# Moving gathered second layers beside the gates, and the second tile's dots beside the dense second layers

## The chip, the cores and the metric

One core of a Trainium2 chip runs the whole program. The metric is the device time of one execution in microseconds (us). A profile of one execution shows what each engine did: TensorE (PE for matmuls, PEld for weight loads), VectorE (DVE), ScalarE (ACT), GpSimd (POOL) and the queues, of which SP loads weights, ACT moves intermediate results, and POOL issues the gathers.

## What is computed

Two transformer blocks run one after the other on 512 tokens of width 1024. The change lies in the last part of the second, a layer that finds single-neuron experts by product keys. Each token has 8 heads with 16 picks each, so 128 experts out of 16384, each with a gate:

```python
def peer_ffn(h, w_query, keys1, keys2, expert_u, expert_v):
    ...
    top_s, top_pos = lax.top_k(cand_s, PEER_TOPK)
    idx = jnp.take_along_axis(cand_i, top_pos, axis=-1)
    gate = jax.nn.softmax(top_s.astype(jnp.float32), axis=-1).astype(h.dtype)
    ...
    def block(args):
        hb, ib, gb = args
        act = jax.nn.gelu(jnp.einsum('thkd,td->thk', expert_u[ib], hb), approximate=False)
        return jnp.einsum('thk,thkd->td', gb * act, expert_v[ib])
```

expert_u and expert_v are 16384 x 1024 in float32, 64 MB each.

## The kernel before, in words

phase_d does this layer. It treats the 512 tokens as four tiles of 128 and in two ways.

Tiles 0 and 1 (NS = 2) are *fetching* tiles. For each token its 128 rows of u are gathered: gather n brings one row of 1024 floats to each of the 128 partitions (L1346), and VectorE multiplies it with the token's own row and sums it into one column of dots (L1355, a "dot"). After 128 dots ScalarE takes Gelu and the product with the gate (L1357, L1358) gives gg. Then the second layer: step r of a tile gathers four sets of rows of v (one for each group of 32 tokens) and multiplies them on the PE with z, which holds gg transposed (L1377, L1378) so that one block of 32 columns picks one token per row (L1384). A tile has 32 such steps of 4 gathers and 8 matmuls; I call them V steps. Their sums stand in two PSUM tiles os.

Tiles 2 and 3 (256 tokens, ND) are *dense*: all 16384 experts are computed. In 128 chunks n, the PE multiplies a chunk of u with the tokens (u_chunk, L1328), ScalarE takes Gelu. The first 68 chunks (JR) stay in SBUF as ge, the other 60 go to DRAM as st and come back as gl. A gate must be multiplied into each; the gates are built from one-hot matrices by VectorE and ScalarE in 64 gate steps (gates, L1299 to L1315), on the PE as small matmuls pg (L1309); the part for st goes to DRAM as gdr. At last, in 128 dense steps, the PE multiplies a chunk with the rows of v of that chunk (L1495) into four PSUM tiles o.

So there are two stages. In the *gates stage* (loop over n) the PE does the chunks of u, pulls the routing of tiles 2 and 3 (rt) until n = 68, then one gate step for each n; beside it the chain ga of both tiles' dots is pulled 200 times in 128 chunks (GU = 200), six more before. Then `early.close()` frees the pools ep and ps, and in the *dense stage* (loop over i) each i does one dense step, pulls one dot until i = 60, and every odd i pulls one V step, 64 in all (rows_left).

The order on each engine comes from a scheduler that simulates the program as it is written down; a generator that is pulled writes its instructions at that point. In the dense stage the PE's order is the written one (manual_schedule). POOL, SP and ACT issue in order, so a gather that waits holds up all behind it. A row buffer is free again when its dot, or its V step, is done: six buffers in pool sb, and six more in pool lp in the dense stage. lp lies in SBUF that ep had, so its tiles wait for what lay there. hr is the residual (tokens before the layer), loaded into one buffer of lp and added by the PE with the identity (residual, L1339), for tiles 2 and 3 inside the first dense step.

Of the kernel before, what the change touches and what calls it, by code (L numbers as in the profile page):

```python
# [11 lines left out]
FT = mybir.dt.float32  # L12
# [11 lines left out]
D = 1024  # L24
# [1091 lines left out]
def phase_d(k):  # L1116
# [14 lines left out]
    with ExitStack() as ctx:  # L1131
# [5 lines left out]
        ps = early.enter_context(tc.tile_pool(name="d_ps", bufs=1, reuse_waits="tile", space=PS))  # L1137
        def pm(tag="a", bufs=3):
            return (pg if tag == "g" else ps).tile([128, 512], FT, name="p" + tag, tag=tag, bufs=bufs)
# [4 lines left out]
        cand = ep.tile([128, 8, 112], FT, name="cand")  # L1144
# [9 lines left out]
        xs = [ep.tile([128, 4, N0], FT, name="xs", tag="kept", bufs=3) for _ in range(2)]  # L1154
# [37 lines left out]
        def first(h, s):  # L1192

            w = k.load(I["peer_wq"][h], [128, 8, 256])
            for side in range(2):
                p = pm()
                for c in range(8):
                    nc.tensor.matmul(p[:, 0:256], w[:, c, 128 * side:128 * side + 128],
                                     x[:, c] if s else xs[c // 4][:, c % 4], start=c == 0, stop=c == 7)
                q = ep.tile([128, 256], FT, name="q", bufs=3)  # L1200
# [13 lines left out]
        def second(j):  # L1214
# [28 lines left out]
            pxf = ep.tile([128, 4, 128], F16, name="pxf", bufs=1)  # L1243
# [6 lines left out]
            res = ep.tile([128, 2, 128], FT, name="res", bufs=2)  # L1250
            yield
            for side in range(2):
                tie, eq = (ep.tile([128, 16, 128], F16, name=n, tag="kept", bufs=3) for n in ("tie", "eq"))
# [34 lines left out]
        def gates(ge):  # L1288
# [3 lines left out]
            for tb in range(NG):  # L1292
                gs = ep.tile([128, 2048], FT, name="gs", tag="big")[:, :JL * TB].rearrange("p (j t) -> p j t", j=JL)
                for t4 in range(TB // 4):
                    t0 = tb * TB + 4 * t4
                    p = pm("g", 2)
                    o1, o2, oh, ol = (ep.tile(sh, F16, name=f"o{n}", bufs=2) for n in range(4))
# [52 lines left out]
        def gathered_u(j):  # L1350

            dots = sb.tile([128, 128], FT, name=f"dots{j}")
            for n in range(128):
                r = gather(I["peer_u_rows"], ia[j][:, n:n + 1])
                stt(r, r, 1.0, ht[j], op0=OP.mult, op1=OP.mult, accum_out=dots[:, n:n + 1])  # L1355
                yield
            act(dots, dots, AF.Gelu)  # L1357
            tt(gg[j], dots, gg[j], op=OP.mult)  # L1358

        def gathered_v(z):  # L1360

            rows = {}

            def fetch(n):
                if n < 32 * NS:
                    o = [32 * g + n % 32 for g in range(4)]
                    rows[n] = [gather(I["peer_v"], iat[n // 32][:, i:i + 1]) for i in o]

            for n in range(2):
                fetch(n)  # L1370
            for n in range(32 * NS):
                j, r = n // 32, n % 32
                fetch(n + 2)
                if r == 0:
                    po = [ps.tile([128, 512], FT, name=f"os{i}", tag=f"os{i}") for i in range(2)]
                    p = pm("g", 2)
                    nc.tensor.transpose(p[:, 0:128], gg[j], k.ident)  # L1377
                    act(z.rearrange("p (g y) -> p g y", g=4)[:, :, 0::33],  # L1378
                        p[:, 0:128].rearrange("p (g r) -> p g r", g=4), AF.Copy)
                rs = rows.pop(n)  # L1380
                for i in range(2):
                    for g in range(4):
                        o = 1024 * g + 32 * r
                        nc.tensor.matmul(po[i][32 * g:32 * g + 32], z[:, o:o + 32], rs[g][:, 512 * i:512 * i + 512],  # L1384
                                         start=r == 0, stop=r == 31, skip_group_check=True)
                if r == 0:
                    residual(po, j)
                if r == 31:
# [25 lines left out]
        rp.append((sb, 6))  # L1414
# [3 lines left out]
        rt, ga = routing(), chain(*(gathered_u(j) for j in range(NS)))  # L1418
        for j in range(NS):
            for _ in second(j):  # L1420
                pass
            pull(ga, 3)
        taken = [0]

        def some(n):
            taken[0] += n
            pull(ga, n)
# [3 lines left out]
        for n in range(JR + JP):  # L1431
# [4 lines left out]
            else:  # L1436
                i = (n - JR) % JG
                if i == 0:
                    while pull(rt, 1):
                        pass  # L1440
                    kept = ep.tile([128, JG, ND], FT, name="kept", bufs=3)
# [4 lines left out]
            pull(ga, (n + 1) * GU // (JR + JP) - n * GU // (JR + JP))  # L1446
# [10 lines left out]
        z = lp.tile([128, 4096], FT, name="z", bufs=1)  # L1457
        nc.gpsimd.memset(z, 0.0)
# [24 lines left out]
        rows_left = gathered_v(z)  # L1483
# [24 lines left out]
        for j in range(4):  # L1508
            y = sb.tile([128, D], FT, name="rows", bufs=6)
# [162 lines left out]
```

## Time and profile before

| what | us |
|---|---|
| median of three runs | 3017.49 (3016.68 to 3018.36) |
| the profiled execution's own time | 3018.37 |
| its span | 3016.6 |
| PE busy | 2713.6 (90%) |
| VectorE busy | 1224.5 (41%) |
| GpSimd busy | 591.7 (20%) |

The shares are means over stages with different limits. The gates stage and the dense stage are the last 1200 us or so, and their stretches must be read one by one: the column PEclk is the clock that was granted to TensorE as a share of full speed, and a DMA share of about 1.0 means that all of the core's 16 DMA engines had packets all the time.

### The profile page before, as it was taken

What the parts mean: (1) busy time and instruction counts of PE and PEld (TensorE: products, weight loads), DVE (VectorE), ACT (ScalarE), POOL (GpSimd) and SP (SyncE); (2) the same over time, 40 slices, a digit from 0 to 9 for tenths busy, and PEclk for the clock granted to TensorE, in tenths of its full rate; (3) what the DMA queues carried; (4) which work ended last, traced back from release to release, by engine and by line L of the source; (5) the groups of instructions that cost most, each with busy time, mean ns of one, the idle gap of its engine ahead of it and who ended that gap; (6) DMA issues with size and microseconds to landing.
All of it is one profiled execution on the core that took longest, in us unless ns stands there. A gap on an engine that the chain in (4) does not pass through costs nothing. (4 is left out here: it accounts for less than half of the span.)

```text
span 3016.6 us, 35266 instructions
## 1 busy us (share of the span) xinstructions
PE 2713.6 (90%) x13794; PEld 1594.1 (53%) x13794; DVE 1224.5 (41%) x3040; ACT 623.2 (21%) x1304; POOL 591.7 (20%) x600
## 2 busy tenths in 40 slices
PE   8999888887888777699999997999998499999997
PEld 6877422322232222377777786888887333333332
DVE  5444411111111111268855389985888522200001
ACT  4333200000000000265333121122555300000000
POOL 1000100000000000000000005454433256544442
PEclk9979999999999999899999998999999699999999
DMA  4104899999999999912113239999999699999996
GB/s 158 42 1 154 367 421 421 421 421 421 420 421 420 421 421 376 376 60 85 56 56 112 92 132 355 365 381 361 379 363 350 225 399 412 412 410 363 401 401 252
DMA packets 185453, 912.93 MB, mean 303 GB/s; under 512 B 18864, under 2 KB 38464, under 8 KB 112192
## 3 DMA queue, kind: packets, MB, share of 16 engines
q1 hardware_dynamic: 83664, 602.85, 49.7%
q0 software_dynamic: 73728, 268.47, 23.0%
q10 hardware_dynamic: 27888, 39.29, 3.6%
q8 instruction: 110, 1.80, 0.2%
q14 instruction: 63, 0.52, 0.0%
HBM read 890.61 MB, written 19.92 MB: 302 GB/s over the span
## 5 line engine op out<-in xcount | busy, mean ns | idle before, releaser
L1328 PE MATMUL pa<-x,w 128*128 128x256 f32 x2048 | 455.4, 381 | 0.0
L1328 PEld LDWEIGHTS pa<-x,w 128*128 128x128 f32 x2048 | 385.9, 191 | 50.6
L1355 DVE SCALAR_TENSOR_TENSOR rows<-rows,ht 128x1024 f32<-128x1024 f32 x256 | 310.5, 1218 | 237.5 <-DMA rows<-in_peer_u_rows,ia 211.4
L1346 POOL DMA_INDIRECT rows<-in_peer_u_rows,ia x256 | 287.8, 1124 | 440.1 <-DVE rows L1355 211.1
L1346 POOL DMA_INDIRECT rows<-in_peer_v,iat x256 | 253.0, 988 | 292.1 <-PE os L1384 151.1
L712 PE MATMUL pr<-w,xs 128*32 128x512 f32 x1024 | 212.4, 697 | 91.6 <-DMA w<-in_expert_up 91.4
L732 PE MATMUL px<-w,ht 128*32 128x512 f32 x1024 | 223.2, 599 | 44.9 <-DMA w<-in_expert_down 35.5
L1495 PE MATMUL o<-w,ge 128*128 128x512 f32 x544 | 243.4, 600 | 0.0
L1495 PE MATMUL o<-w,gl 128*128 128x512 f32 x480 | 215.5, 602 | 4.4 <-DVE gl L1481 4.4
L71 PE MATMUL pm<-xg,w8h 128*128 128x512 f32 x640 | 206.4, 402 | 3.5 <-ACT cc L942 1.4
L712 PE MATMUL pg<-w,xs 128*32 128x512 f32 x1024 | 178.7, 612 | 19.3 <-DMA w<-in_expert_gate 19.3
L960 POOL MEMSET acc<- 128x1024 f32 x1 | 1.0, 952 | 936.4 <-PE px L732 936.4
L712 PEld LDWEIGHTS pr<-w,xs 128*32 128x32 f32 x1024 | 46.0, 124 | 245.1 <-DMA w<-in_expert_up 168.7
L1495 PEld LDWEIGHTS o<-w,ge 128*128 128x128 f32 x544 | 100.8, 191 | 139.4 <-issue 139.4
L732 PEld LDWEIGHTS px<-w,ht 128*32 128x32 f32 x1024 | 53.4, 109 | 203.0 <-DMA w<-in_expert_down 95.8
L718 DVE SCALAR_TENSOR_TENSOR hd<-pr,ga,hd 128x512 f32<-128x512 f32 x16 | 12.0, 751 | 361.6 <-PE pr L712 361.6
L1495 PEld LDWEIGHTS o<-w,gl 128*128 128x128 f32 x480 | 89.4, 191 | 131.0 <-issue 122.9
L1384 PE MATMUL os<-rows,z 128*32 128x512 f32 x1024 | 144.6, 600 | 5.4 <-DMA rows<-in_peer_v,iat 4.3
L1481 DVE TENSOR_TENSOR gl<-gl,g 128x256 f32<-128x256 f32 x60 | 21.5, 420 | 305.2 <-DMA gl<-st 305.2
L71 PEld LDWEIGHTS pm<-xg,w8h 128*128 128x128 f32 x640 | 120.8, 190 | 33.7 <-ACT w8h L59 2.0
L745 DVE TENSOR_TENSOR hT<-hT,po 128x512 f32<-128x512 f32 x128 | 86.0, 687 | 128.7 <-PE po L744 127.3
L59 ACT ACTIVATE w8h<-w 128x1024 fp32r<-128x1024 f32 (+3 forms) x101 | 90.8, 901 | 218.7 <-PE pm L71 106.3
(561 smaller groups left out, 3601.8 us busy)
## 6 DMA issues: line engine op xcount, KB each, us to landing
w<-in_expert_up SPq DMA_DIRECT2D x128, 1024.0 KB, 19.8
w<-in_expert_gate SPq DMA_DIRECT2D x128, 1024.0 KB, 19.8
w<-in_expert_down SPq DMA_DIRECT2D x128, 1024.0 KB, 19.8
w<-in_peer_u SPq DMA_DIRECT2D x64, 1024.0 KB, 8.1
w<-in_peer_v SPq DMA_DIRECT2D x64, 1024.0 KB, 8.3
w<-in_peer_wq SPq DMA_DIRECT2D x16, 1024.0 KB, 4.8
w<-in_w_out SPq DMA_DIRECT2D x8, 1024.0 KB, 4.8
st<-kept ACTq DMA_DIRECT2D x15, 512.0 KB, 9.3
```

The source lines that it names most:

```text
L59: nc.scalar.activation(hi, src, AF.Copy)
L71: nc.tensor.matmul(o, w[:, c, :], x[:, c, s], start=first and c == 0 and n == 0, stop=last and c == kc - 1 and n == 2)
L712: nc.tensor.matmul(p[s], xs[:, 4 * half + c, s], ws[e][:, c], start=half == 0 and c == 0, stop=half == 1 and c == 3, skip_group_check=True)
L718: stt(hd, pu, ga[:, 1:2], hd, op0=OP.mult, op1=OP.mult)
L732: nc.tensor.matmul(pd[n][s], ht[:, 2 * half + f, s], ws[e][:, f, 512 * n:512 * n + 512], start=half == 0 and f == 0, stop=half == 1 and f ...
L745: tt(hx[:, c], hx[:, c], p, op=OP.add)
L1328: nc.tensor.matmul(p[:, :ND], w[:, c], x[:, c], start=c == 0, stop=c == 7)
L1346: nc.gpsimd.indirect_dma_start(out=r, out_offset=None, in_=rows, in_offset=bass.IndirectOffsetOnAxis(ap=idx, axis=0))
L1355: stt(r, r, 1.0, ht[j], op0=OP.mult, op1=OP.mult, accum_out=dots[:, n:n + 1])
L1384: nc.tensor.matmul(po[i][32 * g:32 * g + 32], z[:, o:o + 32], rs[g][:, 512 * i:512 * i + 512], start=r == 0, stop=r == 31, skip_group_chec ...
L1481: tt(b, b, g[:, :, j], op=OP.mult)
L1495: nc.tensor.matmul(out[NS + t][c], w[:, 128 * t:128 * t + 128], vp[:, i % 2, 512 * c:512 * c + 512], start=i == 0, stop=i == NJ - 1, skip_ ...
```

## The change

Dots and V steps become one generator per tile. In the gates stage only tile 0's dots are pulled (128 instead of 200); when they are used up, each odd n pulls a V step of tile 0. What is left of tile 0 is pulled at odd i of the dense stage, beside all dots of tile 1 (one at each i below 16, then two), and from i = 72 on the V steps of tile 1. For that, V steps must run before `early.close()`:

- z becomes four small tiles per tile of tokens, each for eight steps (z_part). In the gates stage they use the places of ion and cand, which routing no longer needs.
- os gets its own PSUM pool, in place of three banks for routing that are closed when routing is done.
- Row buffers: nine in sb (six before); the space comes from fewer buffers elsewhere ("kept" 2 instead of 3; q, pxf, res and the one-hot tiles share eight "k1" tiles); in the dense stage five more in lp, 14 in all (12 before).
- In the gates stage the matmuls of a V step keep their order by a dependency without a semaphore; each step fetches the rows of the next one (ahead = 1; 2 in the dense stage, as before).
- The residual of a fetching tile is added behind its last V step instead of its first.

```diff
-            act(dots, dots, AF.Gelu)
-            tt(gg[j], dots, gg[j], op=OP.mult)
-        def gathered_v(z):
...
+                if n == 127:
+                    act(dots, dots, AF.Gelu)
+                    tt(gg[j], dots, gg[j], op=OP.mult)
                 yield
+        def z_part(j, r8, pool, tag, bufs):
+            z = pool.tile([128, 4, 8, 32], FT, name="z", tag=tag, bufs=bufs)
+            nc.gpsimd.memset(z, 0.0)
+            p = pm("g", 2)
+            nc.tensor.transpose(p[:, 0:128], gg[j], k.ident)
+            act(z.rearrange("p g r y -> p g (r y)")[:, :, r8:r8 + 232:33],
+                p[:, 0:128].rearrange("p (g r) -> p g r", g=4)[:, :, r8:r8 + 8], AF.Copy)
+            return z
+        def gathered_v(j, zt):
+            rows, z = {}, zt["tiles"]
+            def fetch(r):
+                if r not in rows and r < 32:
+                    rows[r] = [gather(I["peer_v"], iat[j][:, 32 * g + r:32 * g + r + 1]) for g in range(4)]
+            po = [os.tile([128, 512], FT, name=f"os{i}", tag=f"os{i}") for i in range(2)]
+            for r in range(32):
+                for n in range(zt["ahead"] + 1):
+                    fetch(r + n)
+                for r8 in (r - r % 8, r - r % 8 + 8):
+                    if (j, r8) not in z and r8 < 32 and r >= r8 - 4:
+                        z[j, r8] = z_part(j, r8, *zt["z"](r8))
...
-        rp.append((sb, 6))
+        rp.append((sb, 9))
...
-        rt, ga = routing(), chain(*(gathered_u(j) for j in range(NS)))
+        zt = {"tiles": {}, "ahead": 1, "held": True, "z": lambda r8: (ep, ("ion", "cand")[r8 // 8 % 2], 1)}
+        rt, ga, gv = routing(), [gathered_u(j) for j in range(NS)], [gathered_v(j, zt) for j in range(NS)]
...
-            pull(ga, (n + 1) * GU // (JR + JP) - n * GU // (JR + JP))
+            if not pull(ga[0], (n + 1) * GU // (JR + JP) - n * GU // (JR + JP)) and n % 2:
+                pull(gv[0], 1)
...
-        rp.append((lp, 6))
+        rp[:] = [(lp, 5)] * 5 + [(sb, 9)] * 9
+        zt["tiles"].clear()
+        zt.update(ahead=2, held=False, z=lambda r8: (lp, "z", 2))
...
-                if i < NJ // 2 - 4:
-                    pull(ga, 1)
                 if i % 2:
-                    pull(rows_left, 1)
+                    pull(gv[0], 1)
+                pull(ga[1], 1 if i < 16 else 2)
+                if i >= 72:
+                    pull(gv[1], (i - 71) * 32 // 56 - (i - 72) * 32 // 56)
```

How the order moves. First POOL, from its first gather on; ia and iat hold the indices for u and v of a tile (the lower number is tile 0), and "x128" is 128 such instructions in a row. Before:

```order
L1346 DMA rows<-in_peer_u_rows,ia_15524 128x1024 x128
L1346 DMA rows<-in_peer_u_rows,ia_15525 128x1024 x79
L1346 DMA rows<-in_peer_v,iat_15526 128x1024 x6
L1458 MEMSET z 128x4096
L1346 DMA rows<-in_peer_u_rows,ia_15525 128x1024
L1346 DMA rows<-in_peer_v,iat_15526 128x1024 x6
L1346 DMA rows<-in_peer_u_rows,ia_15525 128x1024 x2
```

And with the change:

```order
L1348 DMA rows<-in_peer_u_rows,ia_15527 128x1024 x43
L1348 DMA rows<-in_peer_v,iat_15529 128x1024 x41
L1366 MEMSET z 128x1024
L1348 DMA rows<-in_peer_v,iat_15529 128x1024 x32
L1366 MEMSET z 128x1024
L1348 DMA rows<-in_peer_v,iat_15529 128x1024 x35
L1348 DMA rows<-in_peer_u_rows,ia_15528 128x1024 x3
L1348 DMA rows<-in_peer_v,iat_15529 128x1024 x4
L1366 MEMSET z 128x1024 x2
```

Before, the gates stage ended with 79 rows of u for tile 1; now 108 gathers of v for tile 0 stand behind the last row of u for tile 0, and tile 1 begins behind them.

Second, the PE in the middle of the gates stage, from the end of one gate step to the start of another (pa a chunk of u, 8 matmuls; pg a gate step; os a V step). Before:

```order
L1309 LDWEIGHTS o_19730
L1309 MATMUL pg<-o_19733,o_19730 128x128
L1328 MATMUL pa<-x,w 128x256 x36
L1309 LDWEIGHTS o_19771
L1309 MATMUL pg<-o_19773,o_19771 128x128
```

And with the change:

```order
L1311 LDWEIGHTS o_19120
L1311 MATMUL pg<-o_19123,o_19120 128x128
L1391 MATMUL os_18484<-rows,z 32x512 x4
L1391 MATMUL os_18485<-rows,z 32x512 x4
L1330 MATMUL pa<-x,w 128x256 x16
L1391 MATMUL os_18484<-rows,z 32x512
L1330 MATMUL pa<-x,w 128x256 x2
L1311 LDWEIGHTS o_19174
```

V steps now stand between chunks and gates, the first behind chunk 83, the twenty-fifth behind the last chunk; six gate steps are left behind the last chunk, where there were 17.

Third, the PE in the dense stage where tile 1 begins (os_2... the sums of tile 1, o the dense ones, 4 matmuls per dense step). Before, behind dense step 65 (counted from 0):

```order
L1495 MATMUL o_20640<-w,ge_16025 128x512
L1377 MATMUL pg<-cst,gg_15529 128x128
L1384 MATMUL os_21706<-rows,z 32x512 x4
L1384 MATMUL os_21707<-rows,z 32x512 x4
L1339 MATMUL os_21706<-cst,hr 128x128 x4
L1339 MATMUL os_21707<-cst,hr 128x128 x4
L1495 MATMUL o_20637<-w,ge_16025 128x512
```

And with the change, behind dense step 73:

```order
L1507 MATMUL o_20842<-w,gl 128x512
L1368 MATMUL pg<-cst,gg_15532 128x128
L1391 MATMUL os_21765<-rows,z 32x512 x4
L1391 MATMUL os_21766<-rows,z 32x512 x4
L1507 MATMUL o_20839<-w,gl 128x512
L1507 MATMUL o_20840<-w,gl 128x512
```

The transpose of gg needs all dots of tile 1, so the PE comes past this place only when they are done; before, that place came 8 steps earlier, with all but 49 dots done in the gates stage.

## Rows read from the trace of the kernel before

**Rows 1.** Stretches of the last two stages: engines' busy time, clock, DMA.
```profile
core 0: us, PE busy (x) PEld busy (x) DVE busy (x) ACT busy (x) POOL busy (x), PEclk, DMA share, GB/s
2000.00:2080.00 80.00, 80.00 (x373) 70.42 (x372) 48.05 (x82) 9.11 (x24) 48.94 (x41) 1.00 1.01 407
2100.00:2320.00 220.00, 220.00 (x1279) 193.01 (x1278) 183.96 (x413) 118.93 (x374) 83.12 (x72) 1.00 0.95 361
2320.00:2400.00 80.00, 29.76 (x197) 22.96 (x196) 56.45 (x137) 37.03 (x116) 25.42 (x21) 0.61 0.74 250
2400.00:2440.00 40.00, 39.45 (x151) 16.61 (x150) 6.17 (x10) 0.40 (x1) 19.38 (x20) 0.97 0.90 326
2440.00:2660.00 220.00, 216.22 (x706) 76.67 (x705) 53.35 (x87) 0.31 (x1) 131.94 (x130) 1.00 1.02 412
2740.00:2980.00 240.00, 240.00 (x864) 90.89 (x860) 17.21 (x48) 0.00 (x0) 102.16 (x108) 1.00 1.03 398
2980.00:3016.60 36.60, 21.27 (x81) 7.75 (x80) 7.93 (x20) 7.04 (x21) 0.00 (x0) 0.86 0.25 96
```

**Rows 2.** PE timeline at the joint: start, us, engine, line, operation, idle before.
```profile
2320.59 3.24 PE L1328 MATMUL pa<-x,w 128*128 128x256 f32 x14
...
2353.21 1.03 PE L1309 MATMUL pg<-o,o 128*128 128x128 f16 x8 [1.72 <-DVE ge L1315]
...
2373.59 1.01 PE L1309 MATMUL pg<-o,o 128*128 128x128 f16 x8 [2.19 <-DVE ge L1315]
2385.31 3.62 PE L1339 MATMUL o<-cst,hr 128*128 128x128 f32 x16 [10.71 <-DMA hr<-hdr]
...
2397.12 3.78 PE L1339 MATMUL o<-cst,hr 128*128 128x128 f32 x16 [6.47 <-DMA hr<-hdr]
2400.69 4.39 PE L1495 MATMUL o<-w,ge 128*128 128x512 f32 x8
...
2416.45 1.92 PE L1384 MATMUL os<-rows,z 128*32 128x512 f32 x16
2418.30 7.13 PE L1495 MATMUL o<-w,ge 128*128 128x512 f32 x16
2425.37 1.92 PE L1384 MATMUL os<-rows,z 128*32 128x512 f32 x16
```

**Rows 3.** Waits, 2100 to 2320: who waited for whom, total, times, longest.
```profile
POOL rows L1346 <- DVE rows L1355: 147.7, 60, 15.6
```

**Rows 4.** Groups of instructions, 2100 to 2320: busy, mean ns, idle before.
```profile
L1328 PE MATMUL pa<-x,w 128*128 128x256 f32 x919 | 206.4, 381 | 0.0
...
L1355 DVE SCALAR_TENSOR_TENSOR rows<-rows,ht 128x1024 f32<-128x1024 f32 x72 | 86.9, 1219 | 0.0
...
L1346 POOL DMA_INDIRECT rows<-in_peer_u_rows,ia x72 | 83.2, 1156 | 151.4 <-DVE rows L1355 147.7 <-issue 2.8 <-DVE o L1304 0.9
...
L1309 PE MATMUL pg<-o,o 128*128 128x128 f16 x360 | 26.0, 219 | 0.0
```

**Rows 5.** Groups, 2000 to 2080: gathers of rows of u.
```profile
L1346 POOL DMA_INDIRECT rows<-in_peer_u_rows,ia x41 | 50.2, 1223 | 31.4 <-DVE rows L1355 23.4 <-issue 7.9
```

**Rows 6.** Queues and transfers of the whole run: size, us to landing.
```profile
q0 software_dynamic: 73728, 268.47, 23.0%
...
w<-in_peer_v SPq DMA_DIRECT2D x64, 1024.0 KB, 8.3
...
g<-gdr ACTq DMA_DIRECT2D x15, 512.0 KB, 24.9
...
hr<-hdr ACTq DMA_DIRECT2D x4, 512.0 KB, 8.9
```

**Rows 7.** Waits, 2440 to 2660.
```profile
POOL rows L1346 <- DMA rows<-in_peer_v,iat: 49.8, 37, 2.5
...
PEld os L1384 <- DMA rows<-in_peer_v,iat: 20.8, 19, 1.2
```

**Rows 8.** PE timeline, the last V step.
```profile
3003.80 1.92 PE L1384 MATMUL os<-rows,z 128*32 128x512 f32 x16
```

More of the change, by code (lines that the diff above doesn't have):

```diff
@@ L2 @@
 from contextlib import ExitStack
-from itertools import chain
 import numpy as np
@@ L1143, in phase_d @@
         ion = ep.tile([128, 16, 128], F16, name="ion")
-        cand = ep.tile([128, 8, 112], FT, name="cand")
+        cand = ep.tile([128, 8, 128], FT, name="cand")[:, :, 0:112]
         nc.gpsimd.iota(ion, pattern=[[1, 16], [0, 128]], base=0, channel_multiplier=0,
@@ L1152, in phase_d @@
         col_rows(k, rstd, k.rstd)
-        xs = [ep.tile([128, 4, N0], FT, name="xs", tag="kept", bufs=3) for _ in range(2)]
+        xs = [ep.tile([128, 4, N0], FT, name="xs", tag="kept", bufs=2) for _ in range(2)]
         x = sb.tile([128, 8, ND], FT, name="x")
@@ L1249, in second @@
                 nc.vector.copy_predicated(pxf[:, n], pm64, pxf[:, 2 + n])
[L1250 removed]
+            res = ep.tile([128, 2, 128], FT, name="res", tag="k1", bufs=8)
             yield
             for side in range(2):
[L1253 removed]
+                tie, eq = (ep.tile([128, 16, 128], F16, name=n, tag="kept", bufs=2) for n in ("tie", "eq"))
                 act(tie.rearrange("p n (h k) -> p n h k", h=8),
@@ L1296, in gates @@
                     p = pm("g", 2)
-                    o1, o2, oh, ol = (ep.tile(sh, F16, name=f"o{n}", bufs=2) for n in range(4))
+                    o1, o2, oh, ol = (ep.tile(sh, F16, name=f"o{n}", tag="k1", bufs=8) for n in range(4))
                     for n, o in enumerate((o1, o2)):
@@ new lines, in gathered_v @@
+        def gathered_v(j, zt):
[10 more added lines that the diff above has]
+                        z[j, r8] = z_part(j, r8, *zt["z"](r8))
+                rs, last = rows[r], None
@@ L1387, in gathered_v @@
+                        if last is not None and zt["held"]:
+                            tc.add_manual_dep(m.ins, last.ins.name, mybir.DependencyInfo(
+                                mybir.DependencyClass.NoSync, mybir.DependencyReason.DATA), reason="order")
+                        last = m
+                if r == 31:
                     residual(po, j)
-                if r == 31:
                     out[j] = po
@@ L1421, in phase_d @@
                 pass
[L1422 to L1427, printed above, removed]
+            pull(ga[0], 3)
         st = dr.tile([128, JP, ND], FT, name="st")
@@ L1438, in phase_d @@
                 if i == 0:
-                    while pull(rt, 1):
-                        pass
-                    kept = ep.tile([128, JG, ND], FT, name="kept", bufs=3)
+                    if n == JR:
+                        while pull(rt, 1):
+                            pass
+                        ro.close()
+                        os = ctx.enter_context(tc.tile_pool(name="d_os", bufs=1, reuse_waits="tile", space=PS,
+                                                            side="right"))
+                    kept = ep.tile([128, JG, ND], FT, name="kept", bufs=2)
                 u_chunk(n, kept[:, i])
@@ L1499, in phase_d @@
                         residual(out[NS + t], NS + t)
-                if i < NJ // 2 - 4:
-                    pull(ga, 1)
                 if i % 2:
-                    pull(rows_left, 1)
+                    pull(gv[0], 1)
+                pull(ga[1], 1 if i < 16 else 2)
+                if i >= 72:
+                    pull(gv[1], (i - 71) * 32 // 56 - (i - 72) * 32 // 56)
+            for g in gv:
+                while pull(g, 1):
+                    pass
         gain_row = sb.tile([128, D], FT, name="ht1")
@@ L1508, in phase_d @@
         for j in range(4):
-            y = sb.tile([128, D], FT, name="rows", bufs=6)
+            y = sb.tile([128, D], FT, name="rows", bufs=9)
             ss = lp.tile([128, 4], FT, name="ss", bufs=4)
```

35 lines of the change are left out of this document (8 added, 27 removed).

## The prediction, made before the changed kernel was timed

> **What bounds the kernel now.** I read the stretches first [rows 1], then the PE timeline around the joint of the last two stages [rows 2], then waits, groups and transfers. From 2000 on there are two stages. In the gates stage the PE is never idle (80.00 of 80 us from 2000, 220.00 of 220 from 2100) and DMA moves 407 and then 361 GB/s. In the dense stage the PE is near full too, but at 412 and 398 GB/s with a DMA share above 1.0 [rows 1]: there both are limits. Between them lies a hole, 2320 to 2400, with the PE busy 29.76 of 80 us, its granted clock at 0.61 (a mix of the two levels, 1.2 and 2.4 GHz) and DMA at 250 GB/s. Rows 2 show what is in it: the last chunk of u ends at 2323.8, then 17 gate steps stand alone on the PE, waiting for VectorE, until 2374.6; then two loads of hr, and steady dense work only from 2400.7. VectorE was late because it also had 72 dots of 1219 ns between 2100 and 2320 (88 of its 184 us) [rows 1, 4].
>
> So the change is a shift between stages, and its price is read stage by stage: PE time and bytes are the same in sum.
>
> **Gates stage: 25 V steps come in.** By the code, dots of the first tile run out at chunk n = 78, and n = 79, 81, ... 127 pull one V step each: 25 of 32. A V step beside dense work is 1.85 us (2416.45 to 2418.30, at the full clock) [rows 2]: 25 x 1.85 = 46 us on a PE that has no idle time. Eleven more gates stand ahead of the last chunk (6 behind it instead of 17, by the order) at 26.0 us / 45 = 0.58 us: 6 us [rows 4].
>
> Do rows arrive in time? One gather is 268.47 MB / 512 = 0.524 MB, a chunk the same [rows 6]. The first V step stands behind chunk 83. Chunks with their gates pass at 220 us per 57.4 chunks (919 records / 16) [rows 4], 3.83 us; the last 45 take 172, the V steps 46, the extra gates 4: 222 us. In that time come 45 chunks, 92 gathers (12 fewer than 104, since the buffers fill while the V steps wait for their place), 11 st writes and 6 of gdr: some 84 MB, 378 GB/s. The 361 of that stage was no ceiling: POOL waited 147.7 of the 220 us for VectorE to free a row buffer [rows 3]; with the same chunks running, 2000 to 2080 moved 407, a gather per 80/41 = 1.95 us [rows 1, 5]. At 361 the 84 MB take 233 us (+11), at 390 they fit (0, or at best nothing: the PE has no idle time to win). I take +4. The last chunk ends at 2323.8 + 46 + 6 + 4 = 2380.
>
> Row waits inside V steps are in the trace of before, 20.8 us in 19 pieces from 2440 to 2660 [rows 7], and the granted clock there is 1.00 [rows 1]; so I count these 222 us at the full clock. The Trainium skill (TensorE: Matmul & The Clock Gate, section HAM oscillation) speaks against it: a PE that keeps waiting for DMA between its matmuls falls back to the half clock. By that rule the stretch would go towards 444 us; the trace agrees only for waits as long as those of the hole [rows 1, 2]. It is rival E.
>
> **The hole.** VectorE has no dots left beside the gates. Six gates remain; without dots between them nine took 21.4 us (2353.21 to 2374.60) [rows 2], so 6 x 2.4 = 14 us; bounds 0 (gates keep pace with the chunks) and 6 x 3.0 = 18 (17 gates in 50.8 us, with dots). Gates end at 2394. Then hr, twice through one buffer, stays: 2374.6 to 2400.7 = 26 us. Steady dense work starts at 2420, 19 us later than before; in exchange 39 V steps are left instead of 64.
>
> **Dense stage.** PE alone: two dense steps and a V step take 2425.37 - 2416.45 = 8.92 us, so a dense step is 3.535 [rows 2]; 127.3 x 3.535 + 39 x 1.85 + 7 for residuals and the small transposes = 529, an end at 2949. Before, the same sum was 127.3 x 3.535 + 64 x 1.85 + 4 = 572, and it took 2400.7 to 3005.7 = 605 [rows 2, 8]: 33 us lost to DMA. So DMA must be summed too, in two parts, because the second tile's V steps need all 128 of its dots (the transpose of gg stands on the PE behind step 73).
>
> Part one, until the last dot: 128 + 24 gathers 79.7 MB, 37 loads of peer_v 38.8 (four are in the ring already), hr, g and gl 4.2 [rows 6]: 122.7 MB / 412 = 298 us. It can start at about 2386, when the last st write lets the first lp buffers go; for the time until the PE frees V rows I add 10 us (bounds 0 and 25): 2694. VectorE, Gelu and the transposes behind the last dot: 5 us, 2699. The PE reaches that place at 2420 + 73.3 x 3.535 + 7 x 1.85 + 4 = 2696, so both arrive together; the dots cost VectorE 1.2 us each [rows 4], 156 of 300 us, covered.
>
> Part two: 128 gathers 67.1, 23 loads of peer_v 24.1, 13 pairs of g and gl 13.6: 105 MB / 398 = 264 us from 2694: 2958 [rows 1, 6]. The PE needs 54 x 3.535 + 32 x 1.85 + 3 = 253 from 2699: 2952, less. A last V step behind the last rows 3, its residual now behind it 2: 2963. From the last V step to the end 3016.6 - 3005.7 = 10.9 [rows 8]: span 2974. Bounds: at 412 part two is 255 (-9), part one at 398 is 308 (+10).
>
> The rate of this sum is what the trace holds, 412 over 220 us and 398 over 240 [rows 1]. The Trainium skill (DMA: Bandwidth & Descriptors, section Where 436 GB/s comes from) puts about 358 GB/s on transfers between HBM and SBUF. By that figure the 228 MB of the dense stage would take 637 us instead of 562, an end near 3050; the trace does not agree, and only the 361 of the gates stage comes near it. It is rival F.
>
> **The rest at nothing.** Fourteen row buffers: from 2440 to 2660 POOL waited for an earlier gather to land 49.8 us in 37 pieces [rows 7], so two buffers more hide no more there; bounds 0 and the 20.8 us of row waits, which the byte sum already holds. "kept" with two tiles, the shared "k1" tiles and z in the place of ion and cand reorder VectorE before 2000; the PE had fill work there. If one of them holds up a transpose it costs up to 10 us, at best it gives 5. The four small memsets of z take POOL about 1 us each, hidden behind its waits.
>
> Profiled execution: 3018.37 for a span of 3016.6, so 1.8 outside; 2974 + 1.8 = 2976. The median of the runs, 3017.49, lies 0.9 below the profiled one; against it this is -1.4%.
>
> **Rivals.**
> A, the forecast: 2976, own range 2958 to 2996. Chance 0.60.
> B, DMA is the limit throughout, and a new hole eats most of the old. Idle DMA now: (412 - 250) x 80 + (412 - 326) x 40 us = 16.4 MB, 40 us [rows 1]. New: between the last dot of tile 0 (about 2085 at the pace of rows 5, an estimate; nine buffers full by 2100) and chunk 83 (2323.8 - 172 = 2151) only chunks move, 0.524 MB per 3.4 us or 154 GB/s instead of 361: 10.6 MB, 26 us. A gain of 14: 3004. For it: shares above 1.0 in the dense stage. Against: the gates stage is not full (0.95) and DMA idles at the end (96 GB/s from 2980) [rows 1]. Chance 0.18.
> C, the turn to the second tile. POOL issues in order, and rows of u wait for VectorE, which stands before the first products gl until their loads land; V rows behind them are late, and the last dot slips by 30 us with nothing for the PE to do at step 74: 3006. For it: loads of g take 24.9 us to land [rows 6]. Against: only the first three dots stand ahead of those products. Chance 0.12, half of it within 0.2% of no change.
> D, slower. In the gates stage a gather goes on taking 220/72 = 3.06 us [rows 4], now with the PE behind it: 92 x 3.06 = 281 instead of 222 + 4, +55: 3031. It decides from 2.85 us a gather on (92 x 2.85 = 262, 40 us more, and no gain is left). For it: the DMA share of 0.95 there [rows 1]. Against: rows 3 and 5. Chance 0.07.
> E, the waits of the V steps in the gates stage drop the granted clock to 1.2 GHz, as the waits of the hole do: up to 222 us more, 3198. For it: 0.61 in the hole; against: 1.00 with row waits from 2440 on [rows 1, 7]. Chance 0.02.
> F, DMA holds only about the 361 of the gates stage in the dense one: 228 MB / 361 = 632, +70: 3046. For it: that row; against: 412 and 398 [rows 1]. Chance 0.01.
>
> **Numbers.** A measurement of this kernel can tell 0.2% (6 us) from no change. Faster: A 0.60, B 0.18, half of C 0.06: 0.84. Same: the other half of C, 0.06. Slower: D, E and F, 0.10. The range takes A, B and C with the lower bounds (gates -14, part two -9): 2952 to 3012; D to F are left out.
>
> **What would show it.** Right: the last chunk of u ends near 2380 at clock 1.0; behind it some 6 gates and 40 us to steady dense work instead of 77; DMA at 400 or more in the dense stage and V steps of tile 1 from about 2700; the PE's last V step near 2963. Wrong: V steps waiting for rows more than 15 us in sum before 2380 (D); the PE idle more than 15 us at step 74 (C); DMA below 300 between 2100 and 2151 and nothing won at the end (B).

## The result, and the profile after

The changed kernel takes 3040.88 us (median of four runs, 3037.20 to 3047.45) against 3017.09 us for the kernel before in the same session: a ratio of 1.0086, 95% interval 1.0068 to 1.0105. It is 0.9% slower; the forecast was 2976 us and its range ended at 3012 us. The profiled execution took 3037.2 us with a span of 3035.4 us, so its 1.8 us outside the span are as forecast, and the miss is 61 us of span.

The stretches of the last two stages, in the columns of [rows 1]:

```profile
core 0: us, PE busy (x) PEld busy (x) DVE busy (x) ACT busy (x) POOL busy (x), PEclk, DMA share, GB/s
2080.00:2160.00 80.00, 80.00 (x444) 69.08 (x442) 30.70 (x75) 32.57 (x101) 4.93 (x4) 1.00 0.70 247
2160.00:2420.00 260.00, 260.00 (x1458) 168.25 (x1455) 106.66 (x266) 117.81 (x363) 96.86 (x98) 1.00 0.89 324
2420.00:2465.00 45.00, 20.62 (x106) 13.09 (x105) 17.42 (x44) 10.43 (x32) 13.45 (x14) 0.70 0.94 321
2465.00:2540.00 75.00, 74.63 (x266) 30.10 (x266) 23.40 (x38) 1.42 (x3) 44.48 (x42) 1.00 0.96 363
2540.00:2640.00 100.00, 100.00 (x235) 44.36 (x234) 60.45 (x100) 0.00 (x0) 57.70 (x50) 1.00 1.02 413
2730.00:2765.00 35.00, 6.34 (x20) 1.12 (x18) 17.44 (x31) 0.53 (x2) 20.58 (x20) 0.56 1.02 410
2765.00:2960.00 195.00, 193.10 (x706) 72.05 (x706) 14.36 (x40) 0.68 (x3) 87.67 (x94) 1.00 1.03 400
```

The hole of [rows 1] (80 us at 29.76 busy) has shrunk to 45 us at 20.62. But the gates stage now lasts until 2420, with the PE busy in every microsecond of it, and there is a second, new hole at 2730 where tile 1's V steps begin (the turn to tile 1), while DMA runs at 410 GB/s. The PE's timeline shows both (start, us, engine, line, operation, records, idle before); the lines answer to [rows 2, 8]:

```profile
2418.70 1.05 PE L1391 MATMUL os<-rows,z 128*32 128x512 f32 x2
...
2439.68 3.79 PE L1341 MATMUL o<-cst,hr 128*128 128x128 f32 x16 [7.63 <-DMA hr<-hdr]
...
2458.97 3.78 PE L1341 MATMUL o<-cst,hr 128*128 128x128 f32 x16 [13.43 <-DMA hr<-hdr]
2462.55 4.59 PE L1507 MATMUL o<-w,ge 128*128 128x512 f32 x8
...
2467.62 1.92 PE L1391 MATMUL os<-rows,z 128*32 128x512 f32 x16 [0.37 <-ACT z L1369]
...
2710.28 20.76 PE L1507 MATMUL o<-w,gl 128*128 128x512 f32 x48
2752.82 0.45 PE L1368 MATMUL pg<-cst,gg 128*128 128x128 f32 x1 [21.78 <-DVE gg L1360]
...
2762.07 3.30 PE L1391 MATMUL os<-rows,z 128*32 128x512 f32 x10 [6.51 <-DMA rows<-in_peer_v,iat]
...
3020.62 1.92 PE L1391 MATMUL os<-rows,z 128*32 128x512 f32 x16
3022.48 2.05 PE L1341 MATMUL os<-cst,hr 128*128 128x128 f32 x16
```

| place | forecast | measured | late by |
|---|---|---|---|
| last chunk of u ends | 2380 | 2418.7 | 39 |
| steady dense work starts | 2420 | 2462.6 | 43 |
| turn to tile 1 is passed | 2699 | 2765.3 | 66 |
| last V step and its residual end | 2963 | 3024.5 | 62 |
| end of the span | 2974 | 3035.4 | 61 |

So 39 of the 61 us are there when the last chunk ends, and most of the rest arises at the turn. What happened in the gates stage is seen a level closer. This is one of the 25 moved V steps on the PE, cut more often than most (a step is 16 records for its 8 matmuls, two for each):

```profile
2344.18 1.05 PE L1391 MATMUL os<-rows,z 128*32 128x512 f32 x2
2345.15 1.13 PE L1330 MATMUL pa<-x,w 128*128 128x256 f32 x4
2346.21 1.05 PE L1391 MATMUL os<-rows,z 128*32 128x512 f32 x2
2347.19 2.43 PE L1330 MATMUL pa<-x,w 128*128 128x256 f32 x10
2349.54 1.05 PE L1391 MATMUL os<-rows,z 128*32 128x512 f32 x2
2350.52 0.70 PE L1330 MATMUL pa<-x,w 128*128 128x256 f32 x2
2351.05 0.28 PE L1311 MATMUL pg<-o,o 128*128 128x128 f16 x2
2351.26 1.90 PE L1391 MATMUL os<-rows,z 128*32 128x512 f32 x10
```

The scheduler put matmuls of a chunk, and of a gate, between those of the V step. The step is in four pieces; a piece of one matmul takes 1.05 us, the piece of five 1.90 us, 5.05 us in all. A step that stands whole takes 1.92 us, as at 2467.62 above and in [rows 2]. Over 2140 to 2436 the group of the 25 steps (busy us, mean ns of one record, idle before):

```profile
L1391 PE MATMUL os<-rows,z 128*32 128x512 f32 x400 | 81.3, 601 | 0.0
```

81.3 us against the 46 of the forecast. The PE never waited for rows there. It was the gathers that waited for the PE, from the first V step on (POOL's timeline):

```profile
2103.81 1.68 POOL L1348 DMA_INDIRECT rows<-in_peer_v,iat  x1 [19.53 <-DVE rows L1357]
2105.80 0.94 POOL L1348 DMA_INDIRECT rows<-in_peer_v,iat  x1 [0.30 <-issue]
2160.55 0.94 POOL L1348 DMA_INDIRECT rows<-in_peer_v,iat  x1 [53.81 <-PE os L1391]
```

### The profile page after: what moved, and what is told of

Read it like the earlier page. It is cut to its first block, busy times and chain, and to the rows that moved or that the text cites. A ratio compares the mean times of both kernels' runs of the same rounds, so it can differ in the third digit from the quotient of the medians.

```text
span 3035.4 us, 35414 instructions
## 1 busy us (share of the span) xinstructions
PE 2724.2 (90%) x13801; PEld 1591.9 (52%) x13801; DVE 1239.2 (41%) x3040; ACT 627.1 (21%) x1311; POOL 611.0 (20%) x608
## 5 line engine op out<-in xcount | busy, mean ns | idle before, releaser
L1330 PE MATMUL pa<-x,w 128*128 128x256 f32 x2048 | 466.7, 384 | 0.5 <-ACT ge L1331 0.5
L1348 POOL DMA_INDIRECT rows<-in_peer_u_rows,ia x256 | 304.9, 1191 | 325.6 <-DVE gg L1267 109.5
L1507 PE MATMUL o<-w,ge 128*128 128x512 f32 x544 | 237.2, 597 | 0.0
L1391 PE MATMUL os<-rows,z 128*32 128x512 f32 x1024 | 163.1, 607 | 11.6 <-DMA rows<-in_peer_v,iat 10.9
L739 DVE SCALAR_TENSOR_TENSOR yl<-px,ga,yh 128x512 fp32r<-128x512 f32 x32 | 24.0, 751 | 271.0 <-ACT yh L738 269.3
```

Source lines behind the costliest of these rows:

```text
L739: stt(yl[:, o], pd[n], ga[:, 0:1], yh[:, o].bitcast(FT), op0=OP.mult, op1=OP.subtract)
L1330: nc.tensor.matmul(p[:, :ND], w[:, c], x[:, c], start=c == 0, stop=c == 7)
L1348: nc.gpsimd.indirect_dma_start(out=r, out_offset=None, in_=rows, in_offset=bass.IndirectOffsetOnAxis(ap=idx, axis=0))
L1391: m = nc.tensor.matmul(po[i][32 * g:32 * g + 32], z[j, r - r % 8][:, g, r % 8], rs[g][:, 512 * i:512 * i + 512], start=r == 0, stop=False, ...
L1507: nc.tensor.matmul(out[NS + t][c], w[:, 128 * t:128 * t + 128], vp[:, i % 2, 512 * c:512 * c + 512], start=i == 0, stop=i == NJ - 1, skip_ ...
```

## The experiments

Theory 1: a V step that is cut costs what its pieces cost, about 1.05 us for one to four matmuls and 1.9 us for five to eight, and that is the gates stage's loss. Theory 2: from the hole on the DMA engines set the pace until the last dot of tile 1, so the turn waits for bytes. All ratios are to the kernel before, in the same session; sessions differ by some us, so kernels of different sessions are compared by ratio.

| run | median us | ratio | 95% interval |
|---|---|---|---|
| changed kernel | 3040.88 | 1.0086 | 1.0068 to 1.0105 |
| e1 whole V steps | 3003.08 | 0.9952 | 0.9935 to 0.9969 |
| e2 cut after four | 3020.01 | 1.0008 | 0.9995 to 1.0021 |
| e3 cut after three | 3036.97 | 1.0068 | 1.0051 to 1.0085 |
| e4 moves undone | 3017.48 | 1.0000 | 0.9987 to 1.0013 |
| e5 whole, 25 dots beside gates | 3019.16 | 1.0017 | 1.0006 to 1.0027 |
| e6 whole, residual later | 3016.26 | 1.0004 | 0.9990 to 1.0017 |
| e7 e5, e6 and an earlier turn | 3058.97 | 1.0162 | 1.0145 to 1.0179 |
| e8 whole, later turn | 3011.55 | 0.9990 | 0.9973 to 1.0007 |
| e9 e5, all in written order | 2996.49 | 0.9932 | 0.9911 to 0.9953 |
| e10 V steps from chunk 69 | 3012.28 | 0.9975 | 0.9957 to 0.9994 |
| e11 whole, two hr buffers | 3004.49 | 0.9964 | 0.9949 to 0.9978 |
| e12 e10 and two hr buffers | 3009.16 | 0.9975 | 0.9955 to 0.9994 |
| e13 e9 and two hr buffers | 2995.85 | 0.9933 | 0.9919 to 0.9947 |
| e14 e9 without the dots | 3002.72 | 0.9956 | 0.9942 to 0.9970 |

**Whole and cut V steps (e1 to e3).** The order is held by dependencies without semaphores: every matmul of a chunk from n = 68 on, and every one of a V step, stands behind the one before it in the program.

```diff
+        def behind(m):
+            if pe.get("last") is not None:
+                tc.add_manual_dep(m.ins, pe["last"].ins.name, ...)
+            pe["last"] = m
...
-                nc.tensor.matmul(p[:, :ND], w[:, c], x[:, c], ...)
+                m = nc.tensor.matmul(p[:, :ND], w[:, c], x[:, c], ...)
+                if mid:
+                    behind(m)
+                    if c == 0:
+                        mid()
...
+                        if zt["held"] and 4 * i + g == pe["split"]:
+                            yield
```

With split 8 a step stays whole; with 4 or 3 its rest is written down behind the first matmul of the next chunk (mid).

> The eight matmuls of each V step beside the gates stand together, between two chunks of u; nothing else changes. Theory 1 (cut V steps: in the changed kernel a chunk matmul stands inside most V steps, a piece of one to four V matmuls takes 0.98 us of TensorE and a piece of five to eight 1.85 us, so a V step costs some 3.3 us in place of 1.85): the gates stage shortens by about 24 x 1.4 = 34 us, the last chunk of u ends near 2385 us in place of 2418 us, and since the stage after it is full with the same bytes, nearly all of it arrives at the end: 3037 - 33 = 3004 us (2998 to 3012). Rival (rows: the gates stage is long because the gathers of the V rows come late, and the order of TensorE only follows them): TensorE then waits for rows instead, the last chunk stays near 2415 us and the time within 5 us of 3040 us. Second rival (the end is set by the turn to tile 1 alone, whose dots are bound by the DMA engines from a point that the V steps don't set): the last chunk at 2385 us, but the turn's wait grows from 22 us to over 45 us and the time stays above 3025 us.

> As the run with whole V steps, but one matmul of the next chunk of u stands inside each V step, after its first four matmuls (the first half of the columns, all four row groups). Theory 1 with pieces counted in fours: two pieces of four take 2 x 0.98 = 1.96 us in place of 1.85 us, so 24 steps cost 3 us more than whole steps: within 6 us of the whole run, near 3006 us. Rival (each interruption costs about 1 us, wherever it falls): 24 us more than whole, near 3028 us. Rival (rows): no difference to the changed kernel, near 3040 us.

> As the run before it, with the same one chunk matmul inside each V step, but after its first three matmuls. Theory 1 with pieces counted in fours: 0.98 + 1.85 = 2.83 us a step, 24 x 0.98 = 23 us more than whole steps, near 3027 us; against the cut after four it is 20 us more with the same number of interruptions. Rival (each interruption costs about 1 us): the same as the cut after four, within 4 us. Rival (rows): near 3040 us, all three runs alike.

The same view of the PE for the three, one step each, and the group of the same 25 steps over 2140 to 2436. e1:

```profile
2374.80 1.92 PE L1405 MATMUL os<-rows,z 128*32 128x512 f32 x16
...
2384.71 1.92 PE L1405 MATMUL os<-rows,z 128*32 128x512 f32 x16
2386.56 7.17 PE L1338 MATMUL pa<-x,w 128*128 128x256 f32 x32
...
2724.46 0.45 PE L1380 MATMUL pg<-cst,gg 128*128 128x128 f32 x1 [21.06 <-DVE gg L1372]
```
```profile
L1405 PE MATMUL os<-rows,z 128*32 128x512 f32 x400 | 50.2, 598 | 0.7 <-ACT z L1381 0.7
```

e2:

```profile
2375.04 1.06 PE L1405 MATMUL os<-rows,z 128*32 128x512 f32 x8
2376.04 0.70 PE L1338 MATMUL pa<-x,w 128*128 128x256 f32 x2
2376.67 1.06 PE L1405 MATMUL os<-rows,z 128*32 128x512 f32 x8
...
2385.29 1.07 PE L1405 MATMUL os<-rows,z 128*32 128x512 f32 x8
```
```profile
L1405 PE MATMUL os<-rows,z 128*32 128x512 f32 x400 | 57.2, 615 | 0.7 <-ACT z L1381 0.7
```

e3:

```profile
2386.80 1.06 PE L1405 MATMUL os<-rows,z 128*32 128x512 f32 x6
2387.79 0.70 PE L1338 MATMUL pa<-x,w 128*128 128x256 f32 x2
2388.42 1.90 PE L1405 MATMUL os<-rows,z 128*32 128x512 f32 x10
...
2397.87 1.06 PE L1405 MATMUL os<-rows,z 128*32 128x512 f32 x6
```
```profile
L1405 PE MATMUL os<-rows,z 128*32 128x512 f32 x400 | 76.4, 614 | 0.7 <-ACT z L1381 0.7
```

From one step to the next (two chunks, two gates, one V step) it is 9.91 us whole, 10.25 cut after four, 11.07 cut after three. The cut after four costs 0.34 us, more than the 0.11 expected, since the chunk beside it loses too; the same cut one matmul earlier costs 1.16. So theory 1 holds with its count in fours, and the rival that a fixed price for each interruption is all falls: e2 and e3 have equally many cuts, and 17 us of median lie between them, where theory 1 had 20 and the rival at most 4. But e2 by itself missed its forecast. It was to lie within 6 us of e1; the medians lie 17 us apart and the profiled spans 12 (3007.3 and 3019.4). In the same window its V steps take 7.0 us more than those of e1, and its chunks 6.3 us more (195.6 us for 817 records, against 189.3 for 821). An interruption thus has a price of its own beside the count in fours. The rival of late rows falls as well: e1 shortens the gates stage with the same gathers, the last chunk ends at 2393.7 (2385 was expected, and it was 2418.7), and all of it arrives at the end, 3003 us in the middle of what was expected. The wait at the turn stayed at 21 us, so it neither took the gain back nor went away.

Counted with 1.05 us for a piece up to four and 1.90 (whole: 1.92) for a larger one, the orders alone give, against the measured groups: changed kernel 32 and 25 pieces, 81.1 (81.3); e1 2 and 25, 50.1 (50.2); e2 51 and 1, 55.5 (57.2); e3 28 and 24, 75.0 (76.4).

**The moves undone (e4).** Tile 1's dots go back beside the gates and all V steps beside the dense steps; buffers and small tiles stay as changed.

```diff
-            if not pull(ga[0], (n + 1) * GU // (JR + JP) - n * GU // (JR + JP)) and n % 2:
-                pull(gv[0], 1)
+            for _ in range((n + 1) * GU // (JR + JP) - n * GU // (JR + JP)):
+                if not pull(ga[0], 1):
+                    pull(ga[1], 1)
```

> The changed kernel with its moves undone: the dots of both tiles stand in the gates stage again as far as they did before, and all V steps stand in the dense stage, one in every second step; 14 row buffers, the four-part z and the new places of the small tiles stay. All theories that put the loss in the moved V steps and dots: the time of the kernel before, 3017 us within 5 us. Rival (the small parts that were priced at nothing, the buffers and the tiles that now share a tag, cost something): over 3025 us; or the buffers are worth something: under 3008 us.

1.0000 (0.9987 to 1.0013): what the forecast priced at nothing is, in sum, worth nothing.

**The turn (e5, e9, e14, e8).** e5 pulls one dot of tile 1 behind each V step beside the gates. e9 also holds the gates' matmuls and the transposes for z in the written order, by the same `behind`; e14 is e9 without the dots.

```diff
                 pull(gv[0], 1)
+                pull(ga[1], 1)                                  # e5, e9
...
-                            nc.tensor.matmul(p[:, 128 * i:128 * i + 128], o1[:, i], o[:, i], ...)
+                            behind(nc.tensor.matmul(...))       # e9, e14
...
+            if zt["held"]:                                      # z's transpose: e9, e14
+                behind(m)
```

> The run with whole V steps, and after each V step beside the gates one dot of tile 1 is fetched and taken (25 of the 128), in the place of the dense stage. Theory 2 (the turn to tile 1 is bound by the bytes that the DMA engines carry before the last dot: 25 gathers of 524 KB are 13.1 MB, 32 us at the 412 GB/s of that stretch, and the stretch of the gates has room at 361 GB/s): PE's wait for the last dot and the first rows, 21 + 7 us in the whole run, falls to under 8 us, and the time to some 2980 us (2972 to 2990). Rival (the dots beside the gates hold up the gathers and the gates by as much as the turn gains, nine buffers being eight rows of two V steps and one more): the last chunk of u ends after 2410 us in place of 2393 us, time 3000 us or more.

> The run with 25 dots of tile 1 beside the gates, with the matmuls of the gates and the transposes for z held in the written order too, so that none of them stands inside a V step. In the run with the dots, V steps beside the gates took 157 us of TensorE from 2100 us on against 133 us with whole steps, because matmuls of gates stood inside them. Theory 1 (any matmul of another kind inside a V step costs, not only a chunk's): the 24 us come back, 3019 - 24 = 2995 us (2985 to 3002), with no wait over 8 us at the turn. Rival (the dots beside the gates hold TensorE up by themselves, by their share of VectorE, which makes gates late): TensorE waits for the gates' inputs instead, and the time stays at 3010 us or more.

> The run held in the written order, without the 25 dots beside the gates: all 128 dots of tile 1 beside the dense steps, as in the changed kernel. Theory 2 (the dots beside the gates take away the wait at the turn, and pay with gates that come late): the waits at the turn are back at 28 us, the gates' waits fall from 16 us to under 5 us, time near the 3003 us of the run with whole V steps (2998 to 3009). Rival (the gain against the whole run came from the written order, not from the dots): 2996 us or less.

In e5 the wait for the last dot was gone, and yet it missed: the scheduler had put gate matmuls inside the V steps instead (30 small pieces and 25 large, 79.0 us by the count, 80.7 measured). Its time and the end of its last chunk (2429.2) are those of the rival, but the rival's reason is not what is seen: the PE waited only 5.1 us for the gates' inputs. Held in order, the 25 steps are back at 50.6 us and the time at 2996, as theory 1 expected. e5's group, then e9's:

```profile
L1405 PE MATMUL os<-rows,z 128*32 128x512 f32 x400 | 80.7, 614 | 0.7 <-ACT z L1381 0.7
```
```profile
L1407 PE MATMUL os<-rows,z 128*32 128x512 f32 x400 | 50.6, 613 | 1.0 <-ACT z L1383 1.0
```

The PE's waits from 2080 on (total, times, longest) in e9 and then in e14:

```profile
PE o L1353 <- DMA hr<-hdr: 22.4, 2, 11.9
PE pg L1318 <- DVE ge L1325: 12.8, 7, 2.0
PE o L1528 <- DVE gl L1515: 5.4, 1, 5.4
```
```profile
PE o L1353 <- DMA hr<-hdr: 21.5, 2, 13.1
PE pg L1380 <- DVE gg L1372: 21.1, 1, 21.1
PE os L1407 <- DMA rows<-in_peer_v,iat: 11.6, 3, 6.7
```

So 25 dots moved ahead do take away the turn's waits (21.1 + 11.6), and half of it comes back as gates that wait for VectorE. The profiled spans differ by 10 us (2998.7 and 2988.3), the ratios by 0.0024 with intervals that overlap: that the dots gain is likely, not shown. The written order alone gains nothing over e1: e14 is at e1's time.

e8 starts the V steps of tile 1 at dense step 80 instead of 72 and moves no byte:

```diff
-                if i >= 72:
-                    pull(gv[1], (i - 71) * 32 // 56 - (i - 72) * 32 // 56)
+                if i >= 80:
+                    pull(gv[1], (i - 79) * 32 // 48 - (i - 80) * 32 // 48)
```

> The run with whole V steps, with the V steps of tile 1 from the 80th dense step on (32 over 48 steps) in place of the 72nd; no byte and no instruction is added or taken away. Theory 2 (bytes): TensorE fills the 28 us of waiting at the turn with eight dense steps, but the V rows, 67 MB, are then fetched in 8 steps less, and TensorE waits for rows or pieces of peer_v afterwards: time within 8 us of the 3003 us of the whole run. Rival (only the order at the turn is wrong, and the wait is lost TensorE time that a later turn gives back): the waits at the turn fall under 8 us, none takes their place, and the time is 2980 us or less.

```profile
2728.35 22.44 PE L1525 MATMUL o<-w,gl 128*128 128x512 f32 x48 [23.47 <-DVE gl L1512]
```

The PE goes past the old place and waits for gl instead. The wait had been no mistake of order alone: with a ratio of 0.9990 against 0.9952 e8 lies some 11 us above e1, outside the 8 us that were expected of it and far from its rival's 2980 us.

**The hole and an earlier start (e6, e7, e10 to e13).** e6 adds the dense tiles' residual at step 6, e11 gives hr two buffers and the rows 13. e10 pulls tile 0's dots faster (GU = 235) so that 30 V steps stand beside the gates, from chunk 69 on, in the written order; e12 and e13 add the two hr buffers to e10 and e9. e7 is e5 and e6 with the V steps of tile 1 from step 62.

```diff
-                    if i == 0:
+                    if i == 6:                                  # e6, e7
                         residual(out[NS + t], NS + t)
...
-            hr = lp.tile([128, 8, 128], FT, name="hr", bufs=1)
+            hr = lp.tile([128, 8, 128], FT, name="hr", bufs=2)  # e11, e12, e13
-        rp[:] = [(lp, 5)] * 5 + [(sb, 9)] * 9
+        rp[:] = [(lp, 4)] * 4 + [(sb, 9)] * 9                   # e11, e12, e13
...
-    GU = 200
+    GU = 235                                                    # e10, e12
-... and n % 2:
+... and n % 2 and n > JR:                                       # e10, e12
...
+                if i >= 62:                                     # e7
+                    pull(gv[1], (i - 61) * 32 // 66 - (i - 62) * 32 // 66)
```

> The run with whole V steps, with the residual of the two dense tiles added in the seventh dense step and not in the first, so that the two loads of hr (7.5 and 13.5 us of waiting in the hole) lie beside dense steps. Theory 2 (the DMA engines bound everything up to the turn): dense steps begin some 19 us earlier, near 2420 us in place of 2440 us, but the last dot lands only as much earlier as the hole used less than full DMA speed (321 of 412 GB/s over 45 us: 10 us at most), so the wait at the turn grows from 21 us to over 28 us: time 2993 to 3003 us. Rival (TensorE bounds the stretch and the hole is lost in full): the turn's wait stays at 21 us and the time is 2984 us.

> The run with whole V steps, with two buffers for hr, paid for with one row buffer (13 in place of 14): the second load of hr no longer waits for the first one's matmuls. Theory 2 (bytes bound the stretch up to the turn): the wait for hr falls from 21 us to some 8 us, the dense steps begin some 13 us earlier, and the wait at the turn grows by most of it: time 2995 to 3006 us. Rival (the hole is lost TensorE time in full): the turn's wait stays at 21 us, time 2990 us or less.

> Whole V steps with all of TensorE's work beside the gates held in the written order, and tile 0's dots pulled 235 in place of 200 for each 128 chunks, so that V steps begin behind chunk 69 in place of 79 and 30 stand beside the gates in place of 25. Theory 2 (the turn is bound by bytes, and the gap of the DMA engines at 215 GB/s between 2105 and 2155 us lies empty because POOL waits for the first V step): the gap is filled with 5 V steps' rows, 10.5 MB or 25 us at 412 GB/s; the last chunk of u ends 9 us later, near 2403 us, the waits at the turn fall from 28 us to under 10 us, time 2980 us (2972 to 2992). Rival (V steps that early wait for the last dots of tile 0, which the DMA engines deliver no sooner): TensorE waits over 15 us near 2105 us and the time is 2995 us or more.

> Early V steps (30 beside the gates) and two buffers for hr together, 13 row buffers. Theories 1 and 2: with the bytes before the turn reduced by 10.5 MB the hole's 13 us are TensorE's own now, so they come off the end: 10 us below the run with early V steps alone, 2968 us (2960 to 2982). Rival (bytes bound the rest as a whole): within 5 us of the run with early V steps alone.

> The run with 25 dots beside the gates and everything of TensorE held in the written order, with two buffers for hr and 13 row buffers. Theory 2 (once the bytes before the turn are fewer, no wait at the turn takes back what the hole gives): the 22 us of waiting for hr fall to about 10 us and all of that comes off the end: 2996 - 12 = 2984 us (2976 to 2990). Rival (bytes bound the rest as a whole, or another wait takes the place): within 4 us of 2996 us.

> Whole V steps, 25 dots of tile 1 beside the gates, the residual of the dense tiles in the seventh dense step, and tile 1's V steps spread from the 62nd dense step on in place of the 72nd. Theories 1 and 2 together: dense steps begin near 2420 us, and with the bytes before the last dot reduced by 13.1 MB neither the DMA engines nor a wait bounds the rest: 529 us of TensorE and a tail of 11 to 13 us, 2962 us (2952 to 2975). Rival (DMA engines bound the whole of the rest, whose bytes are only moved): no better than the run with the dots alone, within 6 us of it.

e11 came out at the time that theory 2 had (hr's wait fell from 21 to 8.1 us and the time stayed), but the wait at the turn, which was to grow, stayed at 21.8 us. e12 and e13 came out as their rivals, e12 within 5 us of e10 and e13 within 4 us of e9. e6 and e7 missed both sides, and e10 has the time of its rival without the early wait that was to cause it. The traces show part of the reason. In e6 the wait for hr went to step 6, and a new one stood ahead of it; ScalarE's timeline:

```profile
2415.64 10.53 ACTq L1507 DMA_DIRECT2D gl<-st  x1
2426.27 0.23 ACT L1381 ACTIVATE z<-pg 128x32 f32<-128x32 f32 x1 [20.91 <-DMA g<-gdr]
```

The copy into z stands on ScalarE's queue behind the loads of gl that it issues, and the first dense V step waited 13.4 us for it. In e13 the same wait grew from 1.7 to 9.5 us and that for gl from 5.4 to 10.0, while hr's fell from 22.4 to 12.2: nothing gained. e10 did fill the gap (321 GB/s from 2100 to 2160 against 214 in e1) and lost the wait at the turn, but the last chunk ended at 2422.6 in place of the 2403 expected, with the V steps' z transposes waiting for gates (8.8 and 4.6 us) and a granted clock of 0.97 from 2160 to 2400, and hr then took 35 us, for which no row gives the reason:

```profile
PE o L1353 <- DMA hr<-hdr: 35.0, 2, 18.0
```

e7 has e5's cut steps, e6's z wait (14.5 us) and an hr wait of 18.1 us together, and is the slowest. Theory 2 is right that the turn waits for bytes, and wrong in what it promised: taking bytes or a wait away moved the waiting to gates, hr, z or gl. The most that may have arrived at the end is some 7 us by the ratios, in e9 against e14, of 33 us of waiting at the turn.

e9 and e13 beat both kernels, at 0.9932 and 0.9933: 0.7% faster than before, and by the ratios 1.5% below the changed kernel. They are more than the change, since 25 dots of tile 1 stand beside the gates too. The change as it was meant, with whole V steps, is e1 (0.9952) or, in the written order throughout, e14 (0.9956).

## Why the prediction was wrong, point by point

**Gates stage, the step that failed: "25 x 1.85 = 46 us".** The places of the V steps were right, 25 of them, and the PE had no idle time. The price was of a whole step. The order that stood ahead of the prediction, in the second pair of rows, shows a V matmul alone between two stretches of a chunk (x16, x1, x2): the steps were cut, and I counted where they stood, not how. The 25 steps took 81.3 us, 35 more; made whole they took 50.2, and the kernel 3003 us. This is one mis-sized term, and e1 to e3 show it: it alone is the difference between slower and faster. With it falls the premise that "PE time and bytes are the same in sum".

**"I take +4" for late rows** was not needed. The PE did not wait for rows in this stage, and at most 4 us more than the V steps' 35 are left of the 39 by which the last chunk was late; chunk records beside cuts are dearer too (189.5 us for 799 records, against 189.3 for 821 in e1).

**The hole: 40 us, was 44** (2418.7 to 2462.6). The last gates end 13 us behind the last chunk, where 14 were forecast; the two loads of hr then take 30.5 us instead of 26, since the second one took 13.4 us of waiting instead of 6.5 [rows 2]. DMA carried 321 GB/s there.

**Dense stage, part one: "both arrive together" was wrong by the 28 us wait at the turn.** PE's own sum was right to 8 us: from 2462.6 to the place behind step 73 at 2731.0 are 268 us, against 276 forecast. The bytes were late: they start 39 us late with the last chunk, and then DMA did 321 GB/s until 2465 and 363 until 2540, which against 412 loses 10 + 9 us where I had allowed 10. From 2420 to 2720 the gathers waited for V steps too, in one piece of 21.0 us for the step that stood behind the second load of hr:

```profile
POOL rows L1348 <- PE os L1391: 30.5, 3, 21.0
```

So the hole on the PE also held back the bytes that the turn later waited for. Even so this term is worth less than it looks: with the wait gone, e9 is at 2996 and not at 2976.

**Part two** held: 257 us from 2765.3 to the last V step's end at 3022.5, forecast 262, at 400 GB/s; its residual and the tail take 12.9 us, forecast 2 + 10.9.

**Priced at nothing** held (e4).

**The rivals.** D (3031) and F (3046) gave the times nearest, by mechanisms that did not occur. Against D, gathers waited for the PE (198.1 us from 2150 to 2425), not the PE for gathers. B's gap was there, with POOL idle for 53.81 us and 247 GB/s from 2080 to 2160; e10 filled it and won nothing. C's wait at step 74 was there, 22 + 6.5 us, from bytes and not from loads of gl ahead of the dots (from 2420 to 2760 VectorE waited 118.7 us for rows of u and 8.1 us for gl). E did not occur: the clock was 1.00 in the whole gates stage. F neither: 400 to 413 GB/s from 2540 on.

The Trainium skill (TensorE: Matmul & The Clock Gate, section Measured speedup vs the span model) says that small matmuls in different tiles of the array, issued behind one another, take one matmul's time and some 4 ns for each further one. The trace agrees: a piece of one takes 1.05 us and a piece of four 1.06. By that rule a cut V step could have been priced from its pieces, which the sum did not do.

## What to carry to other kernels

When a change moves work next to other work on the same engine, price it as the new order has it: count the pieces in the order, and take each piece's time from a row, not the whole's. Matmuls that run side by side in groups must be kept together in a scheduler's hands, by dependencies or a written order, or one foreign matmul can cost as much as a whole piece of four (here 1.16 us behind the third matmul, against 0.34 behind the fourth). And a wait on the critical path of a kernel whose DMA is full need not be worth its length, as none was here: ask which wait is late next before counting it as gain.

## What the runs showed of the hardware that was not expected

A V step's eight matmuls (two records of about 0.6 us each) take 1.92 us together, and a piece of one to four of them takes the same however many it holds: 1.05, 1.06 and 1.06 us for one, three and four. One chunk matmul inside a step costs 0.34 us behind the fourth and 1.16 us behind the third. Interrupted this way the PE still counts as busy in 260.00 of 260 us at a granted clock of 1.00, so the busy share shows nothing of the loss; the busy time of the group of V steps, at the same count of records, does (81.3 against 50.2 us).
